# Odd mixer: transposed k and second-group q, long attention pieces, TensorE's order by hand

## The chip, the cores and the metric

One core of a Trainium2 chip runs the whole program. The metric is the device time of one execution in microseconds. TensorE multiplies matrices, VectorE and ScalarE work element by element, GpSimd does little here, and SyncE issues the transfers. TensorE's results go to the accumulation memory (PSUM, in banks of 512 fp32 columns) and are brought from there ("evicted") by ScalarE or VectorE.

## The reference, cut to what matters

Two blocks of a transformer run over 256 tokens of width 1024. The second has two layers; each is a half-scaled feed-forward layer, a mixer and another half-scaled feed-forward layer, all with norms ahead and behind. The mixer of the second layer is the odd mixer, with 16 heads of 64:

```python
def odd_mixer(h, w_in, w_out, rel_bias):
    B_, S_ = h.shape[0], h.shape[1]
    q, k, v = jnp.split(h @ w_in, 3, axis=-1)
    q = q.reshape(B_, S_, C_HEADS, HEAD_DIM_2)
    k = k.reshape(B_, S_, C_HEADS, HEAD_DIM_2)
    v = v.reshape(B_, S_, C_HEADS, HEAD_DIM_2)
    return chunk_band_attention(q, k, v, rel_bias) @ w_out
```

chunk_band_attention takes, for each chunk of 64 tokens, the scores against the keys of this chunk and all before it (the 256 tokens fit into the band), multiplies by 1/8, adds a bias that depends on the distance, and uses the softmax to weight the values. h is the residual after an rms norm; its gain g is applied per column, its factor (rstd) per token.

## The kernel before

The tokens are two tiles t of 128. A product in fp32 is three passes on TensorE with operands split into a high and a low part: `mm3` (L270 to L272) multiplies xh by wh, xh by wl and xl by wh into one bank. Ordinary projections have the transposed x as stationary operand and 512 columns of weights as moving one, so they give tokens by columns. The transposed projection `mm3_T` (L358 and L359), used by the feed-forward layers, has a 128x128 piece of wh or wl as stationary operand and moves x of both tiles (256 columns high and 256 low in the first pass, the 256 high ones in the second), so it gives columns by tokens. `cols_T`, a function inside `ffn`, makes 256 columns so: 2 banks of 8 pairs, each evicted by a copy (ScalarE, L467) and a sum (VectorE, L468). The norm's factor is then needed as a row along the tokens (`rstd_rows`, copies L515 and two transposes).

Weights come in blocks of 2048 columns in the order of PLAN, by SyncE into `raw` (3 buffers); ScalarE makes wh (L240) and VectorE wl (L241) in two halves each, which land in 8 buffers. `take` asks for blocks and issues loads and splits ahead.

The odd mixer (L1069) works on two groups of 8 heads. The first group's q and k come by `project2` (tile 0 of q, tile 0 of k, tile 1 of q, tile 1 of k), the others by `project`. q is scaled by the norm's factor and 1/8 on VectorE (L1092), k by the factor on ScalarE (L1094), and `to_T` turns each tile over by four transposes on TensorE (L612) and two copies on ScalarE (L635). `scores` does per tile: the scores of 8 heads (TensorE, L658, two banks `at`), bias and maximum (VectorE, L662), exponential with its sum (ScalarE, L665), transposes of the probabilities (TensorE L685, evicted by ScalarE L688, two banks `tp`), and `inv_rows`: reciprocal (VectorE L704), its spread over 64 columns per head (VectorE copy L705), four transposes (L612) and an eviction (ScalarE, L707). `attend` multiplies probabilities and values (TensorE L727, scaled by VectorE L731). `w_out` is the output projection; `ends` and `finish` apply the norm behind it and write the residual (`xres`, VectorE L400), and `norm_in` turns the residual over for the next layer (TensorE L306, ScalarE L310, VectorE L311 into `xT`).

A scheduler sets the order of every engine by its estimates and the readiness of operands. Only the first mixer (`mixer1`) has TensorE's order by hand: inside `manual_schedule(engines={PE})` TensorE's instructions stay in the order of the code, while the other engines' are still placed by the scheduler. Each engine works through its own list in that order.

## Time and profile before

| | us |
|---|---|
| median of 3 runs | 1324.79 (1324.56 to 1324.92) |
| the profiled execution | 1325.67 |
| its span (first to last instruction) | 1323.9 |
| TensorE busy in the span | 1295.3 |
| VectorE busy | 865.8 |
| ScalarE busy | 739.6 |

The mean granted clock of TensorE was 0.995 of full speed. In a timeline a row has the start, the duration, engine, source line, operation, result <- operands, and shapes. Matmuls overlap in the pipeline, so the distance between two starts tells more than a duration. A bracket at the end gives the idle time of the engine ahead of the row and what ended it. In the rows grouped by line the columns are the count, the summed and the mean duration, and the idle time before with its releasers.

### The profile page before, as it was taken

The page shows a single profiled execution, that of the slowest core. Times are in us where ns is not written, and L with a number is a line of the kernel's source. Part 1 is how long each engine was busy: PE and PEld are TensorE (multiplying, and loading weights), DVE is VectorE, ACT ScalarE, POOL GpSimd, SP SyncE. Part 2 cuts the span into 40 slices and gives each one's busy share as a digit, 9 for nine tenths or more (in the row PEclk, how much of TensorE's full clock was granted, in tenths as well). Part 3 has the DMA queues.
Part 4 walks back from the last instruction along what each step waited for, and adds up shares of the span by engine and source line. Part 5 has one row for each costly group of instructions (what it writes and reads, how often), then busy time and mean ns, then how long its engine had stood idle before and what let it go on. Part 6 is the DMA issues. An engine that isn't in the chain of part 4 may idle for free.

```text
span 1323.9 us, 17937 instructions
## 1 busy us (share of the span) xinstructions
PE 1295.3 (98%) x6932; PEld 1076.6 (81%) x6932; DVE 865.8 (65%) x1400; ACT 739.6 (56%) x1242; POOL 42.4 (3%) x59
## 2 busy tenths in 40 slices
PE   9789999999999999999999999999999999999997
PEld 7567788888888888777888888888888777888886
DVE  6744677745677648896677755777746555777743
ACT  6455655535555436756665544655535855765531
POOL 0310000000000000000000000000001000000000
PEclk9899999999999999999999999999999999999999
DMA  8943555554555554433365554545554452455540
GB/s 354 284 146 119 178 176 187 191 191 163 209 188 188 182 185 166 172 131 124 127 240 188 191 187 166 218 180 191 192 191 175 163 188 103 178 213 188 191 162 32
DMA packets 37510, 238.20 MB, mean 180 GB/s; under 512 B 4272, under 2 KB 7088, under 8 KB 10416
## 3 DMA queue, kind: packets, MB, share of 16 engines
q1 hardware_dynamic: 36064, 234.31, 50.1%
q0 software_dynamic: 640, 2.16, 0.7%
q8 instruction: 54, 0.88, 0.3%
q10 hardware_dynamic: 720, 0.59, 0.1%
q14 instruction: 32, 0.26, 0.1%
HBM read 235.40 MB, written 1.64 MB: 179 GB/s over the span
## 4 chain that ended last, share of the span: by engine, by line
PE 91%; DVE 3%; ACT 2%; DMA 2%; issue 1%; POOL 0%; ACTq 0%; SPq 0%; DVEq 0%; POOLq 0%
PE mm L358 25%; PE mm L272 15%; PE mm L270 15%; PE mm L271 15%; PE mm L359 13%; PE at L658 1%; PE tp L612 1%; DVE wl L241 1%; PE mm L849 1%; PE tp L306 1%; DMA cw<-cw 1%; PE at L727 1%; PE tp L685 1%; PE at L1003 0%; ACT wh L240 0%
## 5 line engine op out<-in xcount | busy, mean ns | idle before, releaser
L241 DVE TENSOR_TENSOR wl<-raw,wh 128x1024 fp32r<-128x1024 f32 (+1 forms) x422 | 508.4, 1219 | 290.9 <-ACT wh L240 283.3
L240 ACT ACTIVATE wh<-raw 128x1024 fp32r<-128x1024 f32 (+1 forms) x422 | 438.7, 1055 | 267.5 <-PE mm L272 150.5
L358 PE MATMUL mm<-xT,wh 128*128 128x512 f32 x1440 | 502.7, 393 | 0.0
L359 PE MATMUL mm<-xT,wl 128*128 128x256 f32 x1440 | 403.9, 280 | 0.0
L358 PEld LDWEIGHTS mm<-xT,wh 128*128 128x128 f32 x1440 | 269.6, 187 | 60.6
L359 PEld LDWEIGHTS mm<-xT,wl 128*128 128x128 f32 x1440 | 272.2, 189 | 0.2
L270 PE MATMUL mm<-wh,slot 128*128 128x512 f32 x536 | 210.0, 392 | 1.3 <-ACT slot L601 1.3
L272 PE MATMUL mm<-wh,slot 128*128 128x512 f32 x536 | 210.3, 392 | 0.6 <-DVE slot L602 0.6
L271 PE MATMUL mm<-wl,slot 128*128 128x512 f32 x536 | 209.5, 391 | 0.0
L270 PE MATMUL mm<-wh,xT 128*128 128x512 f32 (+1 forms) x448 | 177.6, 396 | 1.6 <-ACT xT L342 1.0
L272 PE MATMUL mm<-wh,xT 128*128 128x512 f32 (+1 forms) x448 | 176.7, 396 | 0.1
L271 PE MATMUL mm<-wl,xT 128*128 128x512 f32 (+1 forms) x448 | 175.5, 392 | 0.0
L270 PEld LDWEIGHTS mm<-wh,slot 128*128 128x128 f32 x536 | 100.9, 188 | 22.7 <-ACT slot L601 1.6
L272 PEld LDWEIGHTS mm<-wh,slot 128*128 128x128 f32 x536 | 100.9, 188 | 21.8 <-DVE slot L602 1.0
L271 PEld LDWEIGHTS mm<-wl,slot 128*128 128x128 f32 x536 | 100.9, 188 | 20.6
L467 ACT ACTIVATE slot<-mm 128x256 f32<-128x256 f32 x180 | 66.6, 370 | 67.6 <-PE mm L359 67.6
L270 PEld LDWEIGHTS mm<-wh,xT 128*128 128x128 f32 x448 | 84.8, 189 | 20.0 <-ACT xT L342 1.6
L272 PEld LDWEIGHTS mm<-wh,xT 128*128 128x128 f32 x448 | 84.5, 189 | 17.9 <-DVE xT L311 0.7
L271 PEld LDWEIGHTS mm<-wl,xT 128*128 128x128 f32 x448 | 84.7, 189 | 17.1 <-issue 0.7
L483 ACT ACTIVATE slot<-slot 128x512 fp32r<-128x512 f32 x45 | 28.4, 632 | 93.7 <-DVE slot L481 93.7
L468 DVE TENSOR_TENSOR slot<-slot,mm 128x256 f32<-128x256 f32 x180 | 74.7, 415 | 1.8 <-ACT slot L467 1.8
L310 ACT ACTIVATE xT<-tp,cols 128x128 fp32r<-128x128 f32 x112 | 37.4, 369 | 26.2 <-PE tp L306 15.0
(140 smaller groups left out, 821.3 us busy)
## 6 DMA issues: line engine op xcount, KB each, us to landing
raw<-w SPq DMA_DIRECT2D x209, 1024.0 KB, 4.9
gb<-rows SPq DMA_DIRECT2D x7, 512.0 KB, 5.3
cw<-cw SPq DMA_DIRECT2D x2, 1024.0 KB, 13.8
bias<-rev SPq DMA_DIRECT2D x2, 1024.0 KB, 5.4
xc<-h POOLq DMA_DIRECT2D x4, 394.5 KB, 12.4
first<-first SPq DMA_DIRECT2D x4, 384.0 KB, 4.3
first<-first SPq DMA_DIRECT2D x2, 768.0 KB, 8.1
raw<-w SPq DMA_DIRECT2D x2, 592.0 KB, 4.3
```

Of the source, the lines that this page charges most:

```text
L240: self.nc.scalar.activation(wh[:, o], r[:, i_], AF.Copy)
L241: self.nc.vector.tensor_tensor(wl[:, o], r[:, i_], wh[:, o].bitcast(F32), op=ALU.subtract)
L270: mm(ps, xh, wh, start=start, stop=False)
L271: mm(ps, xh, wl, start=False, stop=False)
L272: mm(ps, xl, wh, start=False, stop=stop)
L306: nc.tensor.transpose(tp[:, j * P : (j + 1) * P], self.xres[t][:, k * P : (k + 1) * P], self.ident)
L310: nc.scalar.activation(xh(k), tp[:, j * P : (j + 1) * P], AF.Copy, scale=g)
L358: mm(bank, wh, x, start=start, stop=False)
L359: mm(bank[:, :256], wl, x[:, :256], start=False, stop=stop)
L467: nc.scalar.activation(zf, bank[:, :256], AF.Copy)
L468: nc.vector.tensor_tensor(zf, zf, bank[:, 256:], op=ALU.add)
L483: nc.scalar.activation(hh, g, AF.Copy)
```

## The change

k of both groups and q of the second are made by `cols_T` (moved out of `ffn`, unchanged), in blocks of 256 columns, and scaled by a product with the row form of the norm's factor (VectorE, L1109 of the new code). Only the first group's q is made as before and turned over by `to_T`, each of its tiles between two of k's halves. The scores of a tile are one piece, those of tile 1 two, put between the matmuls of v's projection (`project_with`, whose dictionary names the k step, from 0 to 7, ahead of which a piece stands); the probabilities and inverse of tile 0 stand there, too. Those of tile 1 and the weight products follow between the halves of the next group's q or, for the second group, inside `w_out`. All of this is inside `manual_schedule` for TensorE; `ends` is called outside.

```diff
-                    b += proj_blocks("odd_w_in_2", (0,), c * 1024 + g * 512, 512)
+                    if g + c == 0 or c == 2:
+                        b += proj_blocks("odd_w_in_2", (0,), c * 1024 + g * 512, 512)
+                    else:
+                        for j in range(2):
+                            b += proj_blocks("odd_w_in_2", (0,), c * 1024 + g * 512 + j * 256, 256)
...
+    def cols_T(self):
+
+        nc = self.nc
+        (b,) = self.take(1)
+        z = self.slot()
+        for f in range(2):
+            bank = self.mmt()
+            for k in range(8):
+                self.mm3_T(bank, k, *self.part(b, k * 256 + f * P, P), k == 0, k == 7)
+            zf = z[:, f * 256 : (f + 1) * 256]
+            nc.scalar.activation(zf, bank[:, :256], AF.Copy)
+            nc.vector.tensor_tensor(zf, zf, bank[:, 256:], op=ALU.add)
+        return z
...
-        self.ends(ps, post, False, nxt)
+        if post is not False:
+            self.ends(ps, post, False, nxt)
+        return ps
...
-        os = []
-        for g in range(2):
-            bias = bias_of(g)
-            res = []
-            both = self.project2((512, 512)) if g == 0 else None
-            for which in range(2):
-                ps = both[which] if both else self.project()
-                dst = [self.slot(), self.slot()]
-                for t in range(2):
-                    q = self.slot()
-                    r = self.rstd[t][:, 0:1]
-                    if which == 0:
-                        nc.vector.tensor_scalar(q, ps[t], r, 0.125, op0=ALU.mult, op1=ALU.mult)
-                    else:
-                        nc.scalar.activation(q, ps[t], AF.Copy, scale=r)
-                    self.to_T(q, dst, t)
-                res.append(dst)
-            sc = self.scores(res[0], res[1], bias)
-            v = self.vcopy(self.project())
-            os.append(self.attend(sc, v))
...
-        self.w_out(part(os[0], 0), part(os[1], 4), post, nxt)
+        heads = list(range(8))
+        os = [[], []]
+
+        def first_q():
+            bs = self.take(2, 2)
+            ps = [self.mmt(), self.mmt()]
+            dst = [self.slot(), self.slot()]
+            for t in range(2):
+                for i, b in enumerate(bs):
+                    self.block_mm(ps[t], b, self.xlhs(t), 0, i == 0, i == 1)
+            qs = []
+            for t in range(2):
+                q = self.slot()
+                nc.vector.tensor_scalar(q, ps[t], self.rstd[t][:, 0:1], 0.125, op0=ALU.mult, op1=ALU.mult)
+                qs.append(q)
+            return qs, dst
+
+        def heads_T(m, mid=None):
+            dst = []
+            for j in range(2):
+                z = self.cols_T()
+                z2 = z[:, :].rearrange("p (f n) -> p f n", f=2)
+                nc.vector.scalar_tensor_tensor(
+                    z2, z2, m, R[:, :256].unsqueeze(1).broadcast_to([P, 2, 256]), op0=ALU.mult, op1=ALU.mult)
+                dst.append(z)
+                if mid is not None:
+                    mid[j]()
+            return dst
+
+        with self.tc.manual_schedule(engines={PE}):
+            left = [lambda: None, lambda: None]
+            for g in range(2):
+                bias = bias_of(g)
+                if g == 0:
+                    qs, qT = first_q()
+                    R = self.rstd_rows()
+                    kT = heads_T(1.0, [lambda: self.to_T(qs[0], qT, 0), lambda: self.to_T(qs[1], qT, 1)])
+                else:
+                    qT = heads_T(0.125, left)
+                    kT = heads_T(1.0)
+                st, pt, rr = [[], []], [{}, {}], [None, None]
+                sm = [self.softmax_rows(t, qT, kT, heads, bias, st[t]) for t in range(2)]
...
+                v = self.vcopy(self.project_with({
+                    2: st[0][0], 4: st[1][0], 6: lambda: (probs(0, heads), inv(0)), 7: st[1][1]}))
...
+                left = [lambda: (probs(1, heads), inv(1)), lambda: (att(0), att(1))]
...
+            ps = self.w_out(part(os[0], 0), part(os[1], 4), False, nxt, {1: left[0], 2: lambda: att(0), 3: lambda: att(1)})
+        self.ends(ps, post, False, nxt)
```

How the order of the engines moves is shown at three places. The same code has line numbers 4 to 8 higher after the change.

TensorE at the start of the odd mixer, before. mm_9051 is q of tile 0, mm_9078 k of tile 0, tp_8986 the turned residual of tile 1:

```order
L271 MATMUL mm_9051<-wl_8858,xT_8939 128x512
L270 MATMUL mm_9078<-wh_9033,xT_8939 128x512
L271 MATMUL mm_9078<-wl_9034,xT_8939 128x512
L272 MATMUL mm_9078<-wh_9033,xT_8939 128x512
L270 MATMUL mm_9078<-wh_9033,xT_8939 128x512
L271 MATMUL mm_9078<-wl_9034,xT_8939 128x512
L272 MATMUL mm_9078<-wh_9033,xT_8939 128x512
L270 MATMUL mm_9078<-wh_9037,xT_8939 128x512
L271 MATMUL mm_9078<-wl_9038,xT_8939 128x512
L272 MATMUL mm_9078<-wh_9037,xT_8939 128x512
L270 MATMUL mm_9078<-wh_9037,xT_8939 128x512
L306 MATMUL tp_8986<-sh,xres_85 128x128 x4
```

The same place after, where mm_9053 is q of tile 0:

```order
L275 MATMUL mm_9053<-wl_8858,xT_8939 128x512
L276 MATMUL mm_9053<-wh_8857,xT_8939 128x512
L274 MATMUL mm_9053<-wh_8857,xT_8939 128x512
L275 MATMUL mm_9053<-wl_8858,xT_8939 128x512
L310 MATMUL tp_8986<-sh,xres_85 128x128 x4
L276 MATMUL mm_9053<-wh_8857,xT_8939 128x512
L274 MATMUL mm_9053<-wh_8863,xT_8939 128x512
L275 MATMUL mm_9053<-wl_8864,xT_8939 128x512
```

The matmuls of k between q's eleventh matmul and the transposes of tile 1's residual are gone; the transposes come right behind it.

TensorE at the first group's scores of tile 1 (at) and probabilities of tile 0 (tp), before:

```order
L270 MATMUL mm_9332<-wh_9339,xT_8939 128x512
L658 MATMUL at_9256<-slot_9173,slot_9153 128x256
L685 MATMUL tp_9229<-sh,e_9205 128x128
L658 MATMUL at_9257<-slot_9173,slot_9153 128x256
L685 MATMUL tp_9229<-sh,e_9208 128x128
L685 MATMUL tp_9229<-sh,e_9211 128x128
L658 MATMUL at_9256<-slot_9173,slot_9153 128x256
L685 MATMUL tp_9229<-sh,e_9214 128x128
L658 MATMUL at_9257<-slot_9173,slot_9153 128x256
L685 MATMUL tp_9236<-sh,e_9217 128x128
L685 MATMUL tp_9236<-sh,e_9220 128x128
L271 MATMUL mm_9332<-wl_9340,xT_8939 128x512
```

After, from the last v matmuls ahead of tile 0's probabilities on (slot_9360 is the spread reciprocal of the inverse):

```order
L275 MATMUL mm_9236<-wl_9177,xT_8939 128x512
L276 MATMUL mm_9236<-wh_9176,xT_8939 128x512
L692 MATMUL tp_9345<-sh,e_9269 128x128
L692 MATMUL tp_9345<-sh,e_9272 128x128
L692 MATMUL tp_9345<-sh,e_9275 128x128
L692 MATMUL tp_9345<-sh,e_9278 128x128
L692 MATMUL tp_9352<-sh,e_9281 128x128
L692 MATMUL tp_9352<-sh,e_9284 128x128
L692 MATMUL tp_9352<-sh,e_9287 128x128
L692 MATMUL tp_9352<-sh,e_9290 128x128
L619 MATMUL tp_9364<-sh,slot_9360 128x128 x4
L274 MATMUL mm_9235<-wh_9180,xT_8939 128x512
```

Scores and probability transposes no longer alternate: the eight transposes stand together, and the four inverse transposes right behind them.

VectorE at the reciprocal (rs) and its spread over the heads (slot) for tile 0 of the first group, before:

```order
L662 ISA mx_9254 128x1
L662 ISA e_9268,mx_9254<-at_9256,bias_9028 128x256
L662 ISA mx_9254 128x1
L704 RECIPROCAL rs_9243<-sm_9194 128x8
L662 ISA e_9271,mx_9254<-at_9257,bias_9028 128x256
L662 ISA mx_9254 128x1
L705 COPY slot_9244<-rs_9243 128x512
L662 ISA e_9280,mx_9254<-at_9274,bias_9028 128x256
```

The same after; e and mx are the biased scores and their maximum, wl a low weight half:

```order
L669 ISA e_9327,mx_9233<-at_9315,bias_9030 128x256
L669 ISA mx_9233 128x1
L669 ISA e_9330,mx_9233<-at_9316,bias_9030 128x256
L669 ISA mx_9233 128x1
L711 RECIPROCAL rs_9359<-sm_9232 128x8
L245 TENSOR_TENSOR wl_9414<-raw_9237,wh_9413 128x1024
L712 COPY slot_9360<-rs_9359 128x512
L245 TENSOR_TENSOR wl_9499<-raw_9305,wh_9498 128x1024
```

Between the reciprocal and its spread copy stood two steps of the maximum; now a weight split stands there, and the next is behind the copy.

## Rows read from the trace of the kernel before

**Rows 1.** The page's busy times: engine, us (share of the span), instructions.

```profile
PE 1295.3 (98%) x6932; PEld 1076.6 (81%) x6932; DVE 865.8 (65%) x1400; ACT 739.6 (56%) x1242; POOL 42.4 (3%) x59
```

**Rows 2.** Timeline of TensorE from the odd mixer's first matmul to the next layer's.

```profile
1012.31 0.39 PE L270 MATMUL mm<-wh,xT 128*128 128x512 f32 x1
...
1014.81 0.39 PE L270 MATMUL mm<-wh,xT 128*128 128x512 f32 x1
...
1017.07 0.64 PE L306 MATMUL tp<-sh,xres 128*128 128x128 f32 x4
...
1022.82 0.39 PE L270 MATMUL mm<-wh,xT 128*128 128x512 f32 x1
...
1034.83 0.39 PE L272 MATMUL mm<-wh,xT 128*128 128x512 f32 x1
...
1132.92 0.39 PE L270 MATMUL mm<-wh,xT 128*128 128x512 f32 x1
```

**Rows 3.** Timeline of TensorE: one piece of four transposes between projection matmuls.

```profile
1072.19 0.60 PE L612 MATMUL tp<-sh,slot 128*128 128x128 f32 x4
...
1072.55 0.48 PE L270 MATMUL mm<-wh,xT 128*128 128x512 f32 x1
...
1072.86 0.40 PE L271 MATMUL mm<-wl,xT 128*128 128x512 f32 x1
```

**Rows 4.** Timeline of TensorE: ends of the first group's scores, transposes and their costliest stretch.

```profile
1039.04 0.71 PE L658 MATMUL at<-slot,slot 64*128 64x128 f32 x8
...
1042.80 0.39 PE L270 MATMUL mm<-wh,xT 128*128 128x512 f32 x1
...
1046.70 0.48 PE L271 MATMUL mm<-wl,xT 128*128 128x512 f32 x1
...
1056.37 0.63 PE L612 MATMUL tp<-sh,slot 128*128 128x128 f32 x4
```

**Rows 5.** Timeline of TensorE in the first mixer: scores, and inverse transposes with their waits.

```profile
84.86 1.13 PE L658 MATMUL at<-slot,slot 64*128 64x256 f32 x8
...
92.77 0.63 PE L612 MATMUL tp<-sh,slot 128*128 128x128 f32 x4 [0.96 <-DVE slot L705]
...
100.83 0.63 PE L612 MATMUL tp<-sh,slot 128*128 128x128 f32 x4 [1.16 <-DVE slot L705]
```

**Rows 6.** Timeline of TensorE in a feed-forward layer: first passes of pairs 1 and 17.

```profile
899.92 0.39 PE L358 MATMUL mm<-xT,wh 128*128 128x512 f32 x1
...
905.47 0.39 PE L358 MATMUL mm<-xT,wh 128*128 128x512 f32 x1
```

**Rows 7.** Timeline of VectorE at the start of the odd mixer.

```profile
1015.32 1.42 DVE L400 SCALAR_TENSOR_TENSOR xres<-slot,pr,xres 128x512 f32<-128x512 f32 x2
...
1016.65 0.61 DVE L311 SCALAR_TENSOR_TENSOR xT<-tp,cols,xT 128x128 fp32r<-128x128 f32 x2
...
1021.26 0.75 DVE L1092 TENSOR_SCALAR slot<-mm,rstd 128x512 f32<-128x512 f32 x1
```

**Rows 8.** Timeline of VectorE in the first mixer, ahead of the inverse at 92.77.

```profile
90.94 1.22 DVE L241 TENSOR_TENSOR wl<-raw,wh 128x1024 fp32r<-128x1024 f32 x1
...
92.20 0.42 DVE L705 COPY slot<-rs 128x512 f32<-128x512 f32 x1
```

**Rows 9.** Grouped by line, whole run: xcount | busy us, mean ns | idle before, releasers.

```profile
L240 ACT ACTIVATE wh<-raw 128x1024 fp32r<-128x1024 f32 x418 | 435.9, 1059 | 267.5 <-PE mm L272 150.5 <-issue 53.3 <-PE mm L358 34.0
...
L468 DVE TENSOR_TENSOR slot<-slot,mm 128x256 f32<-128x256 f32 x180 | 74.7, 415 | 1.8 <-ACT slot L467 1.8
...
L665 ACT ACTIVATE e<-e,mx 128x256 f32<-128x256 f32 x40 | 19.8, 498 | 2.5 <-DVE mx L662 2.5
...
L665 ACT ACTIVATE e<-e,mx 128x128 f32<-128x128 f32 x40 | 15.5, 391 | 4.5 <-DVE mx L662 4.4
...
L688 ACT ACTIVATE slot<-tp 128x512 f32<-128x512 f32 x27 | 15.1, 587 | 4.3 <-PE tp L685 4.1
...
L515 DVE COPY slot<-rstd 128x128 f32<-128x128 f32 x10 | 1.8, 221 | 0.0
```

**Rows 10.** Windows of 4 us in the first mixer: length, busy by engine, PEclk, DMA, GB/s.

```profile
100.00:104.00 4.00, 3.17 (x18) 2.76 (x19) 0.68 (x2) 2.78 (x5) 0.00 (x0) 1.00 0.32 131
104.00:108.00 4.00, 2.07 (x10) 1.23 (x10) 1.83 (x2) 4.00 (x9) 0.00 (x0) 1.00 0.00 0
108.00:112.00 4.00, 4.00 (x14) 2.75 (x15) 0.69 (x1) 1.55 (x4) 0.00 (x0) 0.59 0.78 262
112.00:116.00 4.00, 4.00 (x32) 3.06 (x30) 1.76 (x3) 1.80 (x3) 0.00 (x0) 0.98 0.00 0
```

More of the change, by code (lines that the diff above doesn't have):

```diff
@@ L456, in ffn @@
         pend = (0, 512, hs)
-        def cols_T():
-            (b,) = self.take(1)
-            z = self.slot()
-            for f in range(2):
-                bank = self.mmt()
-                for k in range(8):
-                    self.mm3_T(bank, k, *self.part(b, k * 256 + f * P, P), k == 0, k == 7)
-                zf = z[:, f * 256 : (f + 1) * 256]
-                nc.scalar.activation(zf, bank[:, :256], AF.Copy)
-                nc.vector.tensor_tensor(zf, zf, bank[:, 256:], op=ALU.add)
-            return z
         for c in range(FF_PAIRS):
-            g = cols_T()
+            g = self.cols_T()
             if c == 0:
@@ L479, in ffn @@
                 transposes(pend)
-            u = cols_T()
+            u = self.cols_T()
             nc.vector.tensor_tensor(g, u, g, op=ALU.mult)
@@ L1100, in odd @@
-        part = lambda o, base: lambda t, k: tuple(a[:, (k - base) * P : (k - base + 1) * P] for a in o[t])
-        self.w_out(part(os[0], 0), part(os[1], 4), post, nxt)
+        heads = list(range(8))
[13 more added lines that the diff above has]
+            return qs, dst
@@ new lines, in heads_T, with probs, inv, att @@
+        def heads_T(m, mid=None):
[22 more added lines that the diff above has]
+                sm = [self.softmax_rows(t, qT, kT, heads, bias, st[t]) for t in range(2)]
+                def probs(t, hs, sm=sm, pt=pt):
+                    pt[t].update(self.probs_T(t, sm[t][0], hs))
+                def inv(t, sm=sm, rr=rr):
+                    rr[t] = self.inv_rows(sm[t][1])
+                v = self.vcopy(self.project_with({
+                    2: st[0][0], 4: st[1][0], 6: lambda: (probs(0, heads), inv(0)), 7: st[1][1]}))
+                def att(t, g=g, pt=pt, rr=rr, v=v):
+                    os[g].append(self.attend_t(t, (pt[t], rr[t]), v))
+                left = [lambda: (probs(1, heads), inv(1)), lambda: (att(0), att(1))]
+            part = lambda o, base: lambda t, k: tuple(a[:, (k - base) * P : (k - base + 1) * P] for a in o[t])
+            ps = self.w_out(part(os[0], 0), part(os[1], 4), False, nxt, {1: left[0], 2: lambda: att(0), 3: lambda: att(1)})
```

## The prediction

> **What bounds the kernel now.** I read the busy times first: TensorE is busy for 1295.3 of the 1323.9 us of the span, more than anything else [rows 1]. So the time is the length of TensorE's queue plus the moments in which it stands still, and an engine beside it counts only where TensorE waits for it. Next I read TensorE's own timeline through the odd mixer. Its first projection matmul starts at 1012.31, the first matmul of the feed-forward layer behind it at 1132.92 [rows 2]: the stage is 120.6 us long. Inside it, 53 intervals from 1022.82 to 1034.83 give 0.2267 us from one 512-wide matmul to the next [rows 2]. The stage has 16 blocks of 24 such matmuls, 384 in all: 384 x 0.2267 = 87.1. The other 33.5 us are everything that isn't a weight matmul: about 2.3 for the second tile's norm transposes, about half a microsecond of idle time, and about 30.6 for the transposes, scores and weight products of the two groups of heads. The change works on these 30.6 and on what fills TensorE while it would wait. Now nothing is waited for, since the scheduler breaks the attention into small pieces and puts whatever is ready into TensorE's queue.
>
> **What the change takes away, with TensorE never waiting.**
> First, k of both groups and q of the second are made transposed, so three of four sets of eight transposes vanish: 24, in pieces of four. One piece of four takes 1072.19 to 1072.86 less one matmul, 0.44 [rows 3]. Six of them: **-2.6**. Their evictions go as well, which TensorE doesn't wait for.
> Second, the long pieces. A piece's price is the distance between the matmuls around it less 0.2267. In the first group the pieces with scores, probability transposes and inverse transposes, from the scores at 1039.04 to the inverse transposes at 1056.37 [rows 4] and without the q and k transposes among them, sum to 10.2; the costliest is four score/transpose pairs that alternate, 1042.80 to 1046.70, 3.67 [rows 4]. In long form: a run of eight 256-wide score operations lasts 1.13 in the first mixer, which is ordered by hand already [rows 5], so three runs per group make about 3.5; 24 probability transposes at the 0.11 of the piece of four make 2.6; two inverse pieces of 0.44 make 0.9. That is 7.0, a gain of 3.2 per group, **-6.4** for two. The ends are 2.0 (half of the 1042.80 piece is its own work, not switching) and 4.0 per group. The weight products are one unbroken run before, too: nothing.
>
> **What it adds to TensorE's work.** A transposed block is 32 pairs of a 512-wide and a 256-wide matmul in place of 48 matmuls. Sixteen pairs take 899.92 to 905.47 in the feed-forward layer, 0.347 each [rows 6]. Three quarters of q and k are 96 pairs, 33.3, for 144 matmuls, 32.6: **+0.7**. The row form of the norm factor needs two more transposes and their start: **+0.3**. On the other engines twelve evictions by ScalarE go, and twelve each of a copy, a sum and a row product come; neither stands on the path but where the waits below name it. The weight blocks keep their number and their bytes, so SyncE's queue issues the same loads. So without a wait: -2.6 - 6.4 + 0.7 + 0.3 = **-8.0**.
>
> **What it adds in waits.** TensorE's order is now fixed, so each wait stops everything behind it. The trace of before can't show these waits; I walked each with durations from its rows.
>
> *Start of the mixer.* Before, behind eleven matmuls of q of tile 0 the scheduler put ten matmuls of the first k block into TensorE's queue (the ten mm_9078 rows), and only then the transposes of tile 1's residual. They start at 1017.07 [rows 2], since VectorE ends the residual's two halves at 1015.32 + 1.42 = 1016.74 [rows 7]. After, no k matmul is there: the transposes stand right behind the eleventh matmul, which ends its turn at 1014.81 [rows 2], and the next matmul needs an x half that VectorE writes from 1016.65 on [rows 7]. The wait is 1017.05 - 1014.81 = **2.2**. It could be less only if the residual were ready sooner, and the same VectorE work stands ahead of it.
>
> *Tile 1 of the first q.* Its 24 matmuls now follow at once and need tile 1's sixteen x halves, of which VectorE makes two in 0.61 [rows 7]; between these halves now stand four weight splits of 1.22 [rows 8] and q's scaling of 0.75 [rows 7]. VectorE has 4.9 (sixteen halves) + 4.5 (the splits, which overlap by 0.1 each) + 0.75 + 0.1 = 10.3 us of work from 1016.74 and gets to the last half at about 1027.0; TensorE, with 37 matmuls and four pieces of transposes from 1017.05, wants it at about 1026: wait 0.5 (its last passes need it last). Then come the two transposes for the row form of the norm factor. Their copies, 0.22 each [rows 9], stand on VectorE behind one more split and tile 1's scaling: TensorE is done at about 1027.2, the copies at about 1029.1. Wait **1.9**, so 2.4 together. Nothing covers it, as the transposed k projections stand behind these transposes.
>
> *Inverse of tile 0.* The order on VectorE puts the copy for the inverse transposes behind a weight split (two in the second group) whose ScalarE half stands behind the twelfth exponential. From the start s of the first scores: the split running then ends at s+2.4, the first maximum and hand-over take half a microsecond, eight exponentials at 0.391 [rows 9] end at s+6.0, four of the wider kind at 0.498 [rows 9] at s+7.9; ScalarE's split of 1.06 [rows 9] at s+9.0, VectorE's of 1.22 at s+10.2, the copy of 0.42 [rows 8] at s+10.6. TensorE arrives there after 1.2 (scores), 12 matmuls, 0.2, 1.2 (scores), 12 matmuls and eight transposes at s+9.0. Wait **1.6** in the first group; **2.5** in the second, with another split of about 1.0 ahead. Sum 4.1. Lower end: 0, if the split's ScalarE half slips ahead; upper: one more split each, 6.5.
>
> *Probabilities and inverse of tile 1.* They stand between the first two halves of the next group's transposed q. TensorE wants two banks evicted at 0.587 each [rows 9] while ScalarE still has a split and the projection's eviction ahead: 1.2; then the copy, on VectorE behind a split, the sum of 0.415 [rows 9] and the row product: 0.8. So **2.0**; in the second group, in the output projection, there is no projection to evict: **0.6**. Sum 2.6.
>
> *Score pieces.* Three of the later ones may find a bank still read: 0.2 each, **0.6**, an allowance without a row.
>
> Together: 2.2 + 2.4 = 4.6 at the start, 4.1 and 2.6 around the inverses, 0.6 for the scores, **11.9**; and -8.0 + 11.9 = **+3.9**.
>
> The nearest waits in the trace stand in the first mixer: its inverse transposes waited 0.96 and 1.16 for the same copy [rows 5], with a split right ahead of the copy on VectorE [rows 8]. That supports the mechanism, and says that 1.6 and 2.5 may be too much.
>
> *The clock.* After such waits the granted clock fell once: from 104 to 108 TensorE was busy for 2.07 of 4.00 us, and from 108 to 112 the granted clock was 0.59 [rows 10], the lower of its levels (1.2 of 2.4 GHz) for most of it. That cost 4 x 0.41 = 1.6, with the rest of the next stretch 1.7. The waits at 92 and 100 [rows 5] brought no fall. I take one fall: **+1.7**.
>
> **Sum.** -8.0 + 11.9 + 1.7 = +5.6 us. The profiled execution took 1325.67 (its span of 1323.9 and 1.8 around it); the median is 1324.79, 0.9 lower. 1325.67 + 5.6 - 0.9 = **1330.4**.
>
> **The rivals.**
> *Waits at the first mixer's price.* The four inverse waits cost 1.06 each, the mean of 0.96 and 1.16 [rows 5], in place of 6.7: 4.2. Waits 9.4, no fall of the clock: -8.0 + 9.4 = +1.4, **1326.2**. For it: it is the only measured price of this wait. Against it: there one split stands ahead, here one or two and a row product. Chance 0.26.
> *A fall of the clock behind each long wait.* Five waits (2.2, 1.9, 1.6, 2.5, 2.0) are longer than 1.5; each brings a fall of 1.7 [rows 10]: +3.9 + 8.5 = +12.4, **1337.2**. Against it: the waits of about 1 us at 92 and 100 brought none. Chance 0.12. The Trainium skill, "TensorE: Matmul & The Clock Gate", section "A second HAM failure mode: psum-queue depth-cycling", says that a TensorE which idles briefly between groups of matmuls often enough swings between the lower and the full clock, and pays for warming up between the bursts; by that rule this rival is the forecast. The trace agrees with it for one of the first mixer's waits [rows 10] and not for the two before.
> *The other side: the waits of the softmax vanish.* If ScalarE takes the exponentials at once and the splits later, the copies are there when TensorE arrives: only the start's 4.6 stays, -8.0 + 4.6 = -3.4, **1321.4**, faster. It decides from the point where all waits are below 8.0 - 2.65 = 5.3. For it: VectorE is busy for 865.8 of 1323.9 us [rows 1], so the splits have slack. Against it: both engines work in their written order, and there the splits stand ahead. Chance 0.22.
>
> **How the numbers follow.** The forecast has 0.40, the rivals 0.26, 0.12 and 0.22. About 0.2%, 2.65 us, is what a measurement of this kernel tells from no change. The forecast (+5.6) and the falls (+12.4) are slower: 0.52; the first mixer's price (+1.4) is within: 0.26; the last is faster: 0.22. The range from 1320.5 to 1336.5 goes past the faster case by 0.9, takes in the forecast with 4 us more of waits, and leaves out half of the clock's case and the gains at the high end of the long pieces (two times 0.8 more than taken). The forecast alone would range from 1327.5 to 1334.5 (its waits 3 us fewer or 4 more).
>
> **What would show it.** Stage by stage: 120.6 becomes about 126 from the first q matmul to the next feed-forward matmul. TensorE's idle rows should name VectorE's residual or x halves at the start (about 2.2), VectorE's copy of the norm factor before the two small transposes (1.9), VectorE's copy before the inverse transposes (1.6 and 2.5), and ScalarE's probability eviction (1.2); the granted clock should be below 1 in one stretch. The forecast is wrong if these rows are absent, if the unbroken pieces cost as much as the broken ones, or if the layers around the mixer change, where the order is the same.

## The result, and the profile after

| | before | after |
|---|---|---|
| median, us | 1324.67 (4 runs, 1323.38 to 1324.92) | 1332.22 (4 runs, 1329.11 to 1333.73) |
| ratio, 95% interval | 1 | 1.0057 (1.0045 to 1.0069) |
| the profiled execution | 1325.67 | 1333.73 |
| its span | 1323.9 | 1331.9 |
| odd mixer, first q matmul to next layer's first | 120.61 | 131.70 |

The change makes the kernel slower by 0.57%, some 7.5 us; 1330.4 was forecast. The page of the changed kernel has TensorE no busier than before, in a span that is 8 us longer (compare [rows 1]):

```profile
PE 1293.8 (97%) x6958; PEld 1078.9 (81%) x6958; DVE 872.5 (66%) x1418; ACT 738.3 (55%) x1239; POOL 42.2 (3%) x59
```

So the added time is TensorE standing still, or running at the lower clock (a busy matmul is then longer). The waits of TensorE from 1012 to 1145, grouped: who waits, for whom, us in total, times, longest.

```profile
PE tp L619 <- DVE slot L712: 4.5, 3, 2.3
PE tp L310 <- DVE xT L315: 2.1, 1, 2.1
PE tp L619 <- DVE slot L520: 1.5, 1, 1.5
PE tp L692 <- ACT slot L695: 1.2, 2, 1.0
PE tp L310 <- DVE xres L404: 0.3, 1, 0.3
PE mm L276 <- DVE xT L315: 0.2, 1, 0.2
PE tp L619 <- ACT slot L695: 0.2, 1, 0.2
```

Before, the same view has two rows, 0.3 and 0.2 us. One by one they stand in TensorE's timeline between the two ends of the stage, which answer to the first and the last of [rows 2]:

```profile
1009.29 0.39 PE L274 MATMUL mm<-wh,xT 128*128 128x512 f32 x1
...
1014.00 0.85 PE L310 MATMUL tp<-sh,xres 128*128 128x128 f32 x4 [2.06 <-DVE xT L315]
...
1025.13 0.51 PE L276 MATMUL mm<-wh,xT 128*128 128x512 f32 x1 [0.20 <-DVE xT L315]
...
1027.15 0.46 PE L619 MATMUL tp<-sh,slot 128*128 128x128 f32 x2 [1.51 <-DVE slot L520]
...
1054.60 0.63 PE L619 MATMUL tp<-sh,slot 128*128 128x128 f32 x4 [1.40 <-DVE slot L712]
...
1066.77 1.15 PE L692 MATMUL tp<-sh,e 128*128 128x128 f32 x8 [0.98 <-ACT slot L695]
...
1068.76 0.93 PE L619 MATMUL tp<-sh,slot 128*128 128x128 f32 x4 [0.84 <-DVE slot L712]
...
1105.07 0.63 PE L619 MATMUL tp<-sh,slot 128*128 128x128 f32 x4 [2.25 <-DVE slot L712]
...
1115.17 1.15 PE L692 MATMUL tp<-sh,e 128*128 128x128 f32 x8 [0.25 <-ACT slot L695]
...
1116.51 0.66 PE L619 MATMUL tp<-sh,slot 128*128 128x128 f32 x4 [0.20 <-ACT slot L695]
...
1140.99 0.39 PE L274 MATMUL mm<-wh,xT 128*128 128x512 f32 x1
```

Each stands at a place that the prediction names. The brackets give 2.06 at the transposes of tile 1's residual, 0.20 and 1.51 around the row form of the norm factor, 1.40 and 2.25 at tile 0's inverses, 0.98 and 0.84 at tile 1's probabilities and inverse, 0.25 and 0.20 at the second group's. Windows of 4 us of the same trace (columns as in [rows 10], PEclk third from the end):

```profile
1012.00:1016.00 4.00, 2.00 (x8) 1.71 (x9) 3.93 (x11) 3.84 (x9) 1.70 (x2) 0.79 0.78 290
...
1016.00:1020.00 4.00, 4.00 (x18) 3.21 (x17) 1.94 (x4) 1.06 (x4) 1.39 (x1) 0.78 0.68 230
...
1028.00:1032.00 4.00, 4.00 (x15) 3.39 (x14) 0.36 (x1) 0.04 (x2) 0.00 (x0) 0.58 0.80 297
...
1068.00:1072.00 4.00, 3.25 (x12) 2.89 (x13) 0.61 (x2) 1.14 (x3) 0.00 (x0) 0.62 0.73 262
...
1104.00:1108.00 4.00, 2.93 (x12) 2.06 (x14) 0.93 (x2) 0.89 (x2) 0.00 (x0) 0.81 0.58 238
...
1108.00:1112.00 4.00, 4.00 (x18) 2.85 (x15) 1.47 (x8) 1.99 (x8) 0.00 (x0) 0.76 0.00 0
```

The granted clock falls four times: across 1016 (two half windows), at 1028, at 1068 and across 1108, each time behind one of these waits. A fall costs about 4 x 0.42 = 1.7 us, as in [rows 10]. While it lasts the 512-wide matmuls stand 0.43 us apart in place of 0.2267:

```profile
1015.08 0.63 PE L274 MATMUL mm<-wh,xT 128*128 128x512 f32 x1
1015.50 0.63 PE L275 MATMUL mm<-wl,xT 128*128 128x512 f32 x1
1015.93 0.63 PE L276 MATMUL mm<-wh,xT 128*128 128x512 f32 x1
```

To keep work, waits and clock apart, I use one ledger for all kernels. The stage is the distance between the first q matmul and the next layer's first; waits are all idle times of TensorE in it; the clock's loss is the length of a window (about 3 us) times what is missing from a granted clock of 1, summed; work is what is left. Before: 120.61 = 0.56 + 0 + 120.05. After: 131.70 = 10.03 + 6.82 + 114.85. The work is 5.2 us shorter, the waits are 9.5 and the clock's loss 6.8 longer: +11.1. Since 0.43 is a little less than twice 0.2267, the ledger puts some 0.1 us too much of each fall to the clock, and as much too little to work; for the four falls here that is 0.4 us, and the work is nearer to 115.3. The whole profiled execution is only 8.0 longer since the program ahead of the mixer, which the change leaves alone, took 3.0 less in this execution: the fall of [rows 10] didn't come (1.6), the first block's feed-forward layer was 1.7 quicker at the same granted clock of 1.00, for a reason that stays open, and 0.3 was lost again at the program's start. The part behind the stage is the same, 191.0 and 190.9.

The profiled execution is the slowest of the four and has the lowest mean granted clock: 0.990 at a span of 1331.9, against 0.993, 0.992 and 0.993 at 1329.7, 1331.1 and 1327.3. A thousandth of the clock is 1.3 us over the span. So by an estimate from these clocks the median execution lost 3.3 us more to the clock than the profiled one of before (0.995): about two falls, not four. The clocks are means over the whole program, so this is good to one fall at best. With it the ledger gives -5.2 + 9.5 + 3.3 = +7.6, near the +7.5 of the medians.

### The profile page after: what moved, and what is told of

Same layout as the page of the kernel before. It is cut to its first block, busy times and chain, and to the rows that moved or that the text cites. A ratio compares the mean times of both kernels' runs of the same rounds, so it can differ in the third digit from the quotient of the medians.

```text
span 1331.9 us, 18007 instructions
## 1 busy us (share of the span) xinstructions
PE 1293.8 (97%) x6958; PEld 1078.9 (81%) x6958; DVE 872.5 (66%) x1418; ACT 738.3 (55%) x1239; POOL 42.2 (3%) x59
## 4 chain that ended last, share of the span: by engine, by line
PE 87%; DMA 4%; DVE 4%; ACT 3%; issue 1%; POOL 0%; SPq 0%; ACTq 0%; DVEq 0%; POOLq 0%
PE mm L362 27%; PE mm L363 14%; PE mm L274 14%; PE mm L276 14%; PE mm L275 13%; DMA xc<-h 1%; DVE wl L245 1%; PE at L665 1%; ACT wh L244 1%; PE tp L310 1%; PE tp L619 1%; PE at L734 1%; DMA slot<-cols 1%; PE mm L856 1%; DMA h<-slot 1%
## 5 line engine op out<-in xcount | busy, mean ns | idle before, releaser
L362 PE MATMUL mm<-xT,wh 128*128 128x512 f32 x1536 | 538.0, 394 | 0.0
L363 PE MATMUL mm<-xT,wl 128*128 128x256 f32 x1536 | 431.9, 281 | 0.0
L362 PEld LDWEIGHTS mm<-xT,wh 128*128 128x128 f32 x1536 | 289.0, 188 | 64.0 <-issue 0.2
L363 PEld LDWEIGHTS mm<-xT,wl 128*128 128x128 f32 x1536 | 291.7, 190 | 0.2
L274 PE MATMUL mm<-wh,xT 128*128 128x512 f32 (+1 forms) x400 | 159.7, 399 | 1.5 <-ACT xT L346 0.9
L276 PE MATMUL mm<-wh,xT 128*128 128x512 f32 (+1 forms) x400 | 158.2, 397 | 0.3 <-DVE xT L315 0.2
L275 PE MATMUL mm<-wl,xT 128*128 128x512 f32 (+1 forms) x400 | 157.4, 394 | 0.0
L511 ACT ACTIVATE slot<-mm 128x256 f32<-128x256 f32 x192 | 71.2, 371 | 78.8 <-PE mm L363 78.8
L274 PEld LDWEIGHTS mm<-wh,xT 128*128 128x128 f32 x400 | 76.2, 191 | 19.8 <-issue 2.6
L276 PEld LDWEIGHTS mm<-wh,xT 128*128 128x128 f32 x400 | 76.1, 191 | 16.8 <-DVE xT L315 1.3
L275 PEld LDWEIGHTS mm<-wl,xT 128*128 128x128 f32 x400 | 76.0, 190 | 15.4 <-issue 0.7
L512 DVE TENSOR_TENSOR slot<-slot,mm 128x256 f32<-128x256 f32 x192 | 79.7, 415 | 11.9 <-ACT slot L511 11.9
```

Source lines behind the costliest of these rows:

```text
L274: mm(ps, xh, wh, start=start, stop=False)
L275: mm(ps, xh, wl, start=False, stop=False)
L276: mm(ps, xl, wh, start=False, stop=stop)
L362: mm(bank, wh, x, start=start, stop=False)
L363: mm(bank[:, :256], wl, x[:, :256], start=False, stop=stop)
L511: nc.scalar.activation(zf, bank[:, :256], AF.Copy)
```

## The experiments

All are ratios to runs of the kernel before on the same chip. The ledger is that of each kernel's one profiled execution, in us, while the ratio is that of the medians; the number of falls can differ between the two.

| kernel | stage | waits | clock's loss | work | ratio of times (95%) |
|---|---|---|---|---|---|
| before | 120.61 | 0.56 | 0 | 120.05 | 1 |
| after | 131.70 | 10.03 | 6.82 | 114.85 | 1.0057 (1.0045 to 1.0069) |
| sched | 119.89 | 2.66 | 1.71 | 115.52 | 0.9998 (0.9988 to 1.0008) |
| start | 123.00 | 6.41 | 1.69 | 114.90 | 1.0018 (1.0009 to 1.0028) |
| invlate | 125.61 | 7.61 | 3.39 | 114.61 | 1.0043 (1.0027 to 1.0059) |
| fill | 126.95 | 3.03 | 1.71 | 122.21 | 1.0046 (1.0030 to 1.0061) |
| schedq | 116.07 | 0.60 | 0 | 115.47 | 0.9961 (0.9946 to 0.9977) |
| pieces | 118.24 | 0.67 | 0 | 117.57 | 0.9982 (0.9971 to 0.9993) |
| both | 119.98 | 3.79 | 1.68 | 114.51 | 0.9987 (0.9973 to 1.0000) |
| pool | 124.36 | 7.40 | 1.68 | 115.28 | 1.0012 (0.9996 to 1.0029) |
| startpool | 118.57 | 3.70 | 0 | 114.87 | 0.9979 (0.9960 to 0.9997) |

**sched: the order by hand taken away, all else as changed.**

```diff
-        with self.tc.manual_schedule(engines={PE}):
+        if True:
```

> The transposed projections and all else of the change, but TensorE's order left to the scheduler as before. Theory (waits of the fixed order and the clock's falls behind them make the loss): no wait over 0.5 us and no fall of the granted clock in the odd mixer; transposes saved -2.6, transposed projections +0.7, row form +0.3, pieces as small as before: -1.6 against the kernel before, about 1323 us (1321 to 1325.5). Rival (the transposed projections and what they bring to the other engines cost the time): 1328 us or more, with TensorE busy or waiting for projection evictions.

The time came where it was expected, 1323.54 us, for other reasons than expected. TensorE still waited at the start, and the clock fell behind it:

```profile
1017.14 0.66 PE L310 MATMUL tp<-sh,xres 128*128 128x128 f32 x4 [2.05 <-DVE xT L315]
```

The scheduler had nothing to put there: the transposed k needs both tiles of x, so the ten k matmuls of the old order don't exist. This wait belongs to the transposed projection, not to the order by hand. All others are gone but 0.27 at one inverse, and 0.34 at the stage's end, which is there before as well. The 1.51 ahead of the norm factor's two transposes is gone too, since the scheduler put them, without a wait, between matmuls of the first k block:

```profile
1030.48 0.38 PE L619 MATMUL tp<-sh,slot 128*128 128x128 f32 x2
```

So that wait did belong to the order by hand. And the work was 4.5 us less than before, not 1.6: the scheduler, given the code in the new order, made long pieces, too. What the hand added to that is 115.52 - 114.85 = 0.7 us of work, of which 0.3 is the ledger's share of three more falls, for 7.4 us of waits and 5.1 of clock.

**start: the first q and k as before, ahead of the part ordered by hand.**

```diff
-                    if g + c == 0 or c == 2:
+                    if g == 0 or c == 2:
...
+        both = self.project2((512, 512))
...
-                    qs, qT = first_q()
-                    R = self.rstd_rows()
-                    kT = heads_T(1.0, [lambda: self.to_T(qs[0], qT, 0), lambda: self.to_T(qs[1], qT, 1)])
+                    first = {0: lambda: (self.to_T(qk[0][0], qT, 0), self.to_T(qk[0][1], kT, 0)),
+                             1: lambda: (self.to_T(qk[1][0], qT, 1), self.to_T(qk[1][1], kT, 1)),
+                             3: lambda: rows.append(self.rstd_rows())}
```

> k of the first group made as before together with q, in the scheduler's order; the fixed order begins with v; the row form of the norm factor is made in the midst of v's projection. Theory: the start's waits (2.06, 0.20, 1.51) and two falls of the clock (1.7 each) go, -7.2; eight transposes come back, +0.9, a transposed block's surplus goes, -0.3: -6.6 against the changed kernel, about 1325.6 us (1324 to 1327.5). The waits around the inverses stay at 1.4 and 2.3. Rival (the start's waits are made up for elsewhere, or the falls of the clock come anyway): within 2 us of the changed kernel's 1332.

1326.50 us, as the theory said. The three waits of the start are gone, those around the inverses stand as they were (1.55, 0.98, 0.84, 2.25), and one fall of the clock is left, behind the 2.25.

**invlate: the inverse transposes later.**

```diff
-                    2: st[0][0], 4: st[1][0], 6: lambda: (probs(0, heads), inv(0)), 7: st[1][1]}))
+                    2: st[0][0], 4: st[1][0], 6: lambda: probs(0, heads), 7: st[1][1]}))
...
-                left = [lambda: (probs(1, heads), inv(1)), lambda: (att(0), att(1))]
+                left = [lambda: (inv(0), probs(1, heads[:4])), lambda: (probs(1, heads[4:]), inv(1), att(0), att(1))]
...
-            ps = self.w_out(part(os[0], 0), part(os[1], 4), False, nxt, {1: left[0], 2: lambda: att(0), 3: lambda: att(1)})
+            ps = self.w_out(part(os[0], 0), part(os[1], 4), False, nxt, {1: left[0], 2: lambda: (probs(1, heads[4:]), att(0)), 3: lambda: inv(1), 4: lambda: att(1)})
```

> The changed kernel with the inverse transposes of both tiles put some ten us later in TensorE's order, and tile 1's probability transposes in two halves. Theory: the waits for the spread copy (1.40, 2.25, 0.84) and for evictions of probabilities (0.98, 0.25, 0.20) go, 5.9, and the falls of the clock at 1068 and 1106 with them, 3.4: about 1323 us (1321 to 1326), while the start's waits 2.06 and 1.51 stay. Rival (the waits move to the next place, the weight products or bank evictions): 1329 us or more, with new idle rows at the weight products.

1329.38 us: the theory missed by 6, and the rival's mechanism held in part: the waits moved to other places, though not to the weight products. In the first group tile 1's inverse still waits, longer than in the changed kernel:

```profile
1070.74 0.66 PE L692 MATMUL tp<-sh,e 128*128 128x128 f32 x4 [0.97 <-ACT slot L714]
...
1080.15 0.63 PE L619 MATMUL tp<-sh,slot 128*128 128x128 f32 x4 [2.23 <-DVE slot L712]
```

VectorE's timeline ahead of it shows why:

```profile
1076.69 1.23 DVE L245 TENSOR_TENSOR wl<-raw,wh 128x1024 fp32r<-128x1024 f32 x1 [1.60 <-ACT wh L244]
...
1078.12 1.23 DVE L245 TENSOR_TENSOR wl<-raw,wh 128x1024 fp32r<-128x1024 f32 x1 [0.20 <-ACT wh L244]
...
1079.26 0.41 DVE L512 TENSOR_TENSOR slot<-slot,mm 128x256 f32<-128x256 f32 x1
...
1079.59 0.42 DVE L712 COPY slot<-rs 128x512 f32<-128x512 f32 x1
```

The reciprocal had been ready since 1064.8. But VectorE's order is the scheduler's, and there the copy stands behind these two splits and the sum, close to where TensorE needs it; why the scheduler put it there is not shown. With the consumer moved in a fixed order, the producer moved too. The first group's waits sum to 3.2 as in the changed kernel; only the second group's went, all but 0.25. So 2.4 us of waits went in place of 5.9. The theory's 3.4 for two falls came in the profiled execution, but it was counted from the four falls of one execution; over the six runs the granted clock has a median of 0.992, no better than the changed kernel's.

**fill: the waits filled with matmuls whose result isn't used.**

```diff
+        def fill(n):
+            b = self.mmt() if n else None
+            for _ in range(n):
+                nc.tensor.matmul(b, self.xT[:, :P], self.xT[:, :512], start=True, stop=True)
...
+                    fill(7)
                     R = self.rstd_rows()
...
-                    2: st[0][0], 4: st[1][0], 6: lambda: (probs(0, heads), inv(0)), 7: st[1][1]}))
+                    2: st[0][0], 4: st[1][0], 6: lambda g=g: (probs(0, heads), fill((6, 10)[g]), inv(0)), 7: st[1][1]}))
...
-                left = [lambda: (probs(1, heads), inv(1)), lambda: (att(0), att(1))]
+                left = [lambda g=g: (probs(1, heads[:4]), fill((4, 0)[g]), probs(1, heads[4:]), fill((4, 0)[g]), inv(1)), lambda: (att(0), att(1))]
```

> The changed kernel with idle matmuls, whose result is not used, put on TensorE ahead of four of its waiting places (7 ahead of the norm factor's rows, 6 and 10 ahead of the inverses of tile 0, 4 and 4 around tile 1's probabilities): the places wait as long in time, but TensorE is busy. Theory that the falls of the granted clock come from these idle stretches: the three falls at 1028, 1068 and 1106 go, the one at 1014 stays, 5 us less, with up to 1.5 us lost where a fill is longer than its wait: about 1328 us (1326.5 to 1330). Rival (the falls have another cause): the granted clock still falls three or four times and the time is 1332 us or more.

1329.24 us, within the theory's range. The 31 fillings are 31 x 0.2267 = 7.0 us of work, and the waits are 7.0 less: TensorE got no further, it was only busy. (The ledger's work grows by 7.4; the other 0.3 is its error for three falls.) The clock's loss went from 6.82 to 1.71, and what is left follows the one wait that wasn't filled, at the start:

```profile
1018.80 0.66 PE L310 MATMUL tp<-sh,xres 128*128 128x128 f32 x4 [2.04 <-DVE xT L315]
```

```profile
1016.00:1020.00 4.00, 1.96 (x11) 1.36 (x10) 3.93 (x9) 4.00 (x8) 1.41 (x2) 0.99 0.66 227
...
1020.00:1024.00 4.00, 4.00 (x14) 3.22 (x13) 2.52 (x7) 1.34 (x5) 2.00 (x2) 0.58 0.56 207
```

So in the profiled executions the falls come from the waits, and three of them were worth 5.1 us of the stage. Over the runs the gain is smaller: the granted clocks are 0.992 to 0.995, the changed kernel's 0.990 to 0.993, and the intervals of the two ratios overlap, so the times alone would not show it. The table says the same as the fillings: before, schedq, pieces and startpool, whose longest wait in the stage is 1.13, have no fall there.

**pool: the inverse's copy on GpSimd, whose queue holds no splits.**

```diff
-        self.nc.vector.tensor_copy(
+        self.nc.gpsimd.tensor_copy(
             rb[:, :].rearrange("p (h d) -> p h d", d=64), rs[:, :].unsqueeze(2).broadcast_to([P, 8, 64]))
```

> The changed kernel with the copy that spreads the reciprocals over the heads made by GpSimd, whose queue holds no weight splits (all eight copies of the program, the first mixer's four too). Theory (TensorE waits for this copy because a weight split stands ahead of it on VectorE): the waits 1.40, 0.84 and 2.25 shrink to what the copy takes on GpSimd, by an estimate from a 64x512 fill of 0.52 us there some 0.5 to 1.2, so each to 0.6 or less; with one fall of the clock less about 1328.5 us (1326.5 to 1331). Rival (the sums of the exponentials come late, whoever copies): the waits stay within 0.4 of what they were, about 1332 us.

1326.35 us, just below the theory's range. In the changed kernel VectorE's rows ahead of the wait of 1.40 are these:

```profile
1050.62 0.20 DVE L711 RECIPROCAL rs<-sm 128x8 f32<-128x8 f32 x1
...
1052.89 1.23 DVE L245 TENSOR_TENSOR wl<-raw,wh 128x1024 fp32r<-128x1024 f32 x1 [2.06 <-ACT wh L244]
...
1054.03 0.42 DVE L712 COPY slot<-rs 128x512 f32<-128x512 f32 x1
```

The reciprocal is done at 1050.82; the copy starts at 1054.03, behind a split that waited 2.06 for ScalarE's half, which stands there behind the twelfth exponential. That is the walk of the prediction. With the copy on GpSimd the waits of 1.40, 0.84 and 2.25 are 0.34, 0.29 and 1.13, and now name the eviction of probabilities (the theory had 0.6 or less for each):

```profile
1052.03 0.63 PE L619 MATMUL tp<-sh,slot 128*128 128x128 f32 x4 [0.34 <-ACT slot L695]
...
1065.65 0.63 PE L619 MATMUL tp<-sh,slot 128*128 128x128 f32 x4 [0.29 <-ACT slot L695]
...
1099.36 0.63 PE L619 MATMUL tp<-sh,slot 128*128 128x128 f32 x4 [1.13 <-ACT slot L695]
```

So the copy's place behind the split is shown as the cause of most of these waits. In the 1.13 that is left, ScalarE's eviction starts at 1098.64, behind a weight split of ScalarE's own. The edit also moves the first mixer's copies, which the theory names but doesn't count in its time. There the waits of 0.96 and 1.16 [rows 5] shrink to 0.23 and to nothing, and that mixer, from its first scores to its output projection, takes 31.3 in place of 33.1 us:

```profile
93.09 0.63 PE L619 MATMUL tp<-sh,slot 128*128 128x128 f32 x4 [0.23 <-ACT slot L695]
```

So 1.8 us of the gain over the changed kernel aren't the odd mixer's; without them the time would be about 1328.2, where the theory had 1328.5.

**startpool: the edits of start and of pool together, the order still by hand.**

```diff
+        both = self.project2((512, 512))
...
+        self.nc.gpsimd.tensor_copy(
```

> The run with the first q and k as before (start) with the copy on GpSimd, too. Theory: of its waits 1.55, 0.98 + 0.84 and 2.25 the copy's shrink to 0.6 or less each and the probabilities' 0.98 stays; waits in the stage about 3.0 in place of 6.4, no fall: stage about 118 us in place of 123, the time about 1322 us (1320.5 to 1324.5). Rival (sums late): waits and time as in that run, ratio to before 1.002.

1320.97 us, ratio 0.9979, 2.8 us less than before: the edits add up, with no fall of the clock in the stage and waits of 3.70. With the start's waits gone and the copy's shorter, the stage by hand is 2.0 us shorter than before in the profiled execution. But of the 2.8 us in time 1.8 come from the copies in the first mixer (31.3 for 33.1, as in pool), and what is left, some 1 us, is not clear of noise. So it isn't shown that the odd mixer's order by hand makes the whole kernel faster.

**both: start and invlate together.**

```diff
+        both = self.project2((512, 512))
...
+                    2: st[0][0], 4: st[1][0], 6: lambda: probs(0, heads), 7: st[1][1]}))
```

> TensorE's order by hand from v of the first group on, with both earlier edits: the first q and k as before in the scheduler's order, and the inverses later. Theory: the two edits add up, waits left 0.97 and 2.23 around the inverses of the first group and 0.6 elsewhere, one fall of the clock: stage 114.7 + 3.8 + 1.7 = 120, about 1323 us (1321 to 1325.5). Rival (a hand order without the waits is worth more than the scheduler's): below 1320 us.

1324.39 us; the waits are 0.97 and 2.23 and the small ones, and the stage 119.98, as worked out.

**pieces: only the code's order of the attention, all projections as before, TensorE by the scheduler.** q and k of both groups are made and turned over as before; scores, probabilities, inverses and weight products stand in the code where the change puts them.

```diff
-        with self.tc.manual_schedule(engines={PE}):
+        if True:
...
-                    qT = heads_T(0.125, left)
-                    kT = heads_T(1.0)
+                    for which, dst in enumerate((qT, kT)):
+                        ps = self.project()
...
+                            self.to_T(z, dst, t)
+                        if which == 0:
+                            left[0]()
+                    left[1]()
```

> All q and k made as before, the scheduler orders TensorE, and only the code's order of the scores, probabilities, inverses and weight products is that of the changed kernel. Theory (the order in the code alone makes the pieces long, and that is about 2.9 of the 4.5 us of work that the scheduler's run saved; the transposed projections are the other 1.6): about 1320.6 us (1319.5 to 1322). Rival (the transposed projections make the whole gain): within 0.2% of before, 1323.5.

1322.69 us, ratio 0.9982. The time lies between the theory's range, which ended at 1322, and the rival's 1323.5, and the ratio is still within the rival's 0.2%: the times don't decide between them, but the ledger does. The stage is 2.4 us shorter, with 2.5 us less work, while no projection is changed. So the code's order alone makes long pieces and a gain, a little less than the 2.9 of the theory.

**schedq: start's projections, the changed code's order, TensorE by the scheduler.** It is start without its `manual_schedule`:

```diff
+        both = self.project2((512, 512))
...
-        with self.tc.manual_schedule(engines={PE}):
+        if True:
```

> The scheduler orders TensorE, the first group's q and k are made as before, the second group's q and k transposed, and the pieces stand in the code as in the changed kernel. Theory: the work of the run with the scheduler (115.5 us without waits and falls) plus eight transposes 0.9 less 0.3, no start wait and no fall: stage about 116.7 against 120.6, so about 1319.5 us (1318 to 1321.5), faster than both kernels. Rival (what the scheduler's run gained it gained by idling at the start, or the pieces break up again): 1322.5 us or more.

1319.61 us, ratio 0.9961 (0.9946 to 0.9977): faster than both kernels. Two rows bound its stage, 116.07 us; its only waits are 0.26 and 0.34:

```profile
1009.84 0.39 PE L274 MATMUL mm<-wh,xT 128*128 128x512 f32 x1
...
1037.19 1.16 PE L665 MATMUL at<-slot,slot 64*128 64x128 f32 x16
...
1041.48 1.13 PE L665 MATMUL at<-slot,slot 64*128 64x256 f32 x8
...
1093.56 0.63 PE L619 MATMUL tp<-sh,slot 128*128 128x128 f32 x4 [0.26 <-DVE slot L712]
...
1125.91 0.39 PE L274 MATMUL mm<-wh,xT 128*128 128x512 f32 x1
```

The scores of tile 0 are one run of sixteen, those of four heads of tile 1 one of eight, with no order by hand. start differs from it in that order alone: 123.00 against 116.07, of which waits are 5.8, the clock 1.7, and the work 0.6 less. startpool, without a fall like schedq, also has 0.6 us less work than it: that is what the order by hand brings in work beyond the scheduler's.

## Why the prediction was right, and where it was not

**The bound and the direction.** TensorE's queue bounds the kernel, and the waits in it decide: right. The loss of 7.5 us is on the side and within the range that was given.

**The start: right.** 2.2 was forecast and 2.06 came; 0.5 and 1.9 were forecast, 0.20 and 1.51 came. That nothing can cover the first of them is shown by sched, where the scheduler couldn't either. "Nothing covers it" was said of the 1.9, though, and that holds for the order by hand alone: in sched the two transposes come later and don't wait.

**The inverses: right.** 1.6 and 2.5 against 1.40 and 2.25, 1.2 and 0.8 against 0.98 and 0.84, 0.6 against 0.45. pool shows the split ahead of the copy as the cause, which the walk named. The first mixer's price of 1.06, the rival's, holds for none of the waits of tile 0. The allowance of 0.6 for score pieces wasn't needed; no run has a wait at the scores. In all, 11.9 were forecast and 9.7 came (the 0.34 at the stage's end, which is there before as well, left out).

**The work: the term of the long pieces was too large.** -8.0 was forecast, -5.2 measured. The transposes saved are right: six pieces of four are gone. Where the prediction has 7.0 for one group's scores, probabilities and inverses in long form, after's pieces of the first group, less their waits, are 1.18 + 1.32 + 1.16 for the scores, 1.42 for tile 0's eight probability transposes and its inverse, and 2.76 for tile 1's sixteen and its inverse: 7.8. So 0.8 per group of the mis-size is in the long pieces; the rest is that the old ones sum to 10.0 rather than 10.2, and that the two transposes of the norm factor with their start cost 0.5, not 0.3. With these sizes the sum is -2.6 - 4.3 + 0.7 + 0.5 = -5.7; the last 0.5, or 0.9 without the ledger's error, is spread over small gaps that I didn't follow. Two readings of the prediction are off without weight in the sum: the walk to tile 0's copy adds up to s+10.7, not 10.6, and the second tile's norm transposes take 1.7 by the distances of the matmuls around them, not 2.3.

**The clock: one fall was forecast, four came in the trace.** This is the step that failed: "I take one fall". The profiled execution lost 6.8 us to the clock in the stage, where 1.7 were in the sum; the median one lost about 3.3, by the estimate from the granted clocks. The rival with a fall behind each long wait, given 0.12, is the nearest to the four falls of the trace, though its time of 1337.2 didn't come, and fill shows that the waits are the cause. By the Trainium skill, "TensorE: Matmul & The Clock Gate", section "A second HAM failure mode: psum-queue depth-cycling", short idle times between groups of matmuls make the clock swing where they come often enough; the trace agrees with it here, four falls in 131.7 us. Not each wait is followed by one, though: over the eleven traces, of the fourteen waits of 1.4 to 2.3 us (1.40, 1.51, 1.55 and so on, in after, sched, start, invlate, fill, both and pool) ten were followed by a fall and four were not. A wait of 2.23 has stood on both sides (invlate, both), and so has the start's (2.06 in after, 2.08 in pool). That the number of falls varies between executions of one kernel is what the granted clocks of the changed kernel say, 0.990 to 0.993: the ends differ by 4 us, two falls or so. One more fall in after stands behind two shorter waits, 0.98 and 0.84. What decides whether a wait is followed by a fall stays open.

**How the sum came out near.** That it did is luck in part. For the stage +5.6 was forecast and +11.1 came in the profiled execution: work +2.8 over the forecast, waits 2.4 under, the clock 5.1 over. The errors of the work and of the waits nearly cancel. For the median the clock is, by the estimate above, only some 1.6 over, one fall, and +5.6 + 2.8 - 2.4 + 1.6 = +7.6 is close to the measured +7.5.

**What the change was worth without its waits.** The rival on the other side, in which the waits of the softmax vanish, was worked out at -3.4 with the start's waits kept. The mechanism doesn't act in the kernel as changed, but sched and schedq show what is behind it: sched keeps the start's wait, and with the fall behind it ends where before ends; schedq has neither, and gains 0.39%. Against pieces (0.18%) it also shows what the second group's transposed projections bring: 2.1 us less work.

## What to carry to other kernels

An order by hand on one engine fixes the moment of each consumer, while the producers' engines keep an order that someone else made: read from the written order of both what stands ahead of each producer, and add up that queue in durations of the trace. Long unbroken pieces came here from the order of the code alone; the scheduler kept them and filled the waits. Before a transposed form replaces a plain one, ask what it needs ready at once: here it needed both tiles, and took away the only work that could fill a wait.

## What was new about the hardware

A wait of 1.5 to 2.3 us cost about twice its length where the granted clock fell behind it, 1.7 us on top, and a wait as long in the execution of another kernel cost nothing more (2.23 in invlate, 2.08 in pool). GpSimd's copy of 128x512 from a spread operand took 0.67 us on average (1.07 once), against 0.42 on VectorE, and was still the better place, as no split stood ahead of it. The rows of pool, grouped over the whole run and the longest one in the timeline:

```profile
L712 POOL COPY slot<-rs 128x512 f32<-128x512 f32 x8 | 5.4, 671 | 97.6 <-DVE rs L711 97.6
```

```profile
1062.65 1.07 POOL L712 COPY slot<-rs 128x512 f32<-128x512 f32 x1
```

In three of the eleven traces (before, pieces and both) the transposed pairs of the first block's feed-forward layer ran at 0.353 us each, in the other eight at 0.347 ([rows 6] are of a later layer), at a granted clock of 1.00, over some 95 us. The program is the same up to there, but for the copies in pool and startpool. What slowed them wasn't found. Forty pairs lie between the two rows of before, and between the two of after:

```profile
178.86 0.40 PE L358 MATMUL mm<-xT,wh 128*128 128x512 f32 x1
...
192.99 0.40 PE L358 MATMUL mm<-xT,wh 128*128 128x512 f32 x1
```

```profile
177.33 0.39 PE L362 MATMUL mm<-xT,wh 128*128 128x512 f32 x1
...
191.20 0.39 PE L362 MATMUL mm<-xT,wh 128*128 128x512 f32 x1
```
